# Three unused tiles that move the big tiles' addresses in a hybrid mixer and expert-choice kernel

## The chip, the cores and the metric

The kernel runs on one core of a Trainium2 chip. The metric is the device time of one execution in microseconds (us), the median of several.

## The reference

One layer of a latent backbone: 2048 tokens of 1024 channels, float32 throughout. A modulation vector comes from `c`; then a gated short convolution (the "mixer") and sixteen SwiGLU experts, each of which picks its own 256 tokens.

```python
m_l = (silu(c) @ ada_w + ada_b)
sh1, sc1, g1, sh2, sc2, g2 = jnp.split(m_l, 6, axis=-1)
hl  = rms_norm(x, norm_g[0]) * (1 + sc1) + sh1
gate_b, gate_c, v = jnp.split(hl @ w_in, 3, axis=-1)             # 1024 -> 3 x 1024
lat = x + g1 * ((gate_b * dwconv3(gate_c * v, conv)) @ w_out)
h2  = rms_norm(lat, norm_g[1]) * (1 + sc2) + sh2
aff = softmax(h2 @ w_router)                                     # 16 experts
g, idx = top_k(aff.T, 256)
xs  = h2[idx]                                                    # per expert 256 x 1024
ys  = ((silu(xs @ w_gate) * (xs @ w_up)) @ w_down) * g
out = lat + g2 * scatter_add(ys, idx)
```

## The kernel before

Every large product is made of three passes of TensorE in the type fp32r: an operand is split into a high part (a rounded copy, made by ScalarE) and a low part (what is left, a subtraction on VectorE), and high x high, high x low and low x high are added up in PSUM. In a matmul one operand is stationary (loaded into the array by a weight load, 128 columns here), the other is moving (streamed through it, one column after another).

**Weights.** All weights come in pieces of 512 KB. SyncE's queue loads a piece into one of three `raw` buffers (line 182), ScalarE writes the high half of a `ws` tile (L198), VectorE the low half (L208). There are 8 `ws` tiles of 8192 bytes a partition.

**Start** (0 to 50 us of the span). Columns of `ada_w` are loaded into `hl` buffers (L399), x into `xt` buffers, the first weights in halves (L226).

**Input projection** (to about 600 us), `in_mm`, lines 436, 437 and 439: two passes over 8 channel tiles, in each two quarters of the tokens, and for each of 8 slices `k` nine matmuls: 2 x 8 x 2 x 8 x 9 = 2304 of 512 columns. Moving is the token tile `hl`, stationary is a 128-column slice of `ws`.

**Output projection** (to about 825 us), `out_mm`, lines 641, 642 and 644: 16 token blocks x 8 slices x 6 = 768 matmuls of 512 columns. Here `ws` is moving, and stationary is `hl` (the `vh` and `vl` of the code take buffers of the tag `hl`). In its shadow stands the router (`router_mm`, lines 708 and 709): 32 weight columns of `rts`, 128 moving columns of `hl`.

**Routing** (825 to about 970 us) is a chain of small steps on VectorE, ScalarE and TensorE.

**Experts** (to the end). `gate_up`, lines 1010, 1012 and 1014: per expert 384 matmuls of 256 columns, moving is `xT` (the gathered tokens, transposed), stationary is `ws`; 6144 in all. `down`, lines 1032 to 1034: per expert 96 matmuls of 512 columns, moving is `ws`, stationary is `hT`; 1536 in all.

**Where tiles lie.** A pool gives its tiles places in each partition of the on-chip memory, one behind another in the order in which their names first appear, each rounded up to 32 bytes. The pools stand in the order `consts`, `weights` (`raw`, `ws`), `small`, `mix`. `mix` holds `junk`, `carry`, then 16 buffers `hl` of 4096 bytes, 9 of the tag `b4` (`xt`, `aw`, `u`) of 4096, and 5 of the tag `m2` of 2080. When the mixer is done, the pools `route` and `moe` take the place of `mix`; `moe` begins with `ax` (two of 320 bytes), then `oh`, `xs`, `xT`, `hT`, `sg` and `ot`. No line of the kernel asks for an alignment. The instructions are issued in the order of the code; nothing schedules them anew.

Of the kernel before, what the change touches and what calls it, by code (L numbers as in the profile page):

```python
# [7 lines left out]
F32 = mybir.dt.float32  # L8
# [8 lines left out]
P = 128  # L17
# [23 lines left out]
def block_kernel(ctx: ExitStack, tc, x, c, ada_w, ada_b, norm_g, w_in, conv, w_out, router, wg, wu, wd, out):  # L41
    nc = tc.nc
    ctx.enter_context(tc.manual_schedule())
    consts = ctx.enter_context(tc.tile_pool(name="consts", bufs=1))
# [13 lines left out]
    nc.vector.tensor_scalar(identf, jp, 0.0, None, op0=ALU.is_equal)  # L58
    ones_f = consts.tile([P, P], F32, name="ones_f")
    nc.vector.memset(ones_f, 1.0)  # L60
    spacer = consts.tile([1, 1], F32, name="spacer")
    mhalf = consts.tile([P, 1], F32, name="mhalf")
    nc.gpsimd.memset(mhalf, -0.5)
# [284 lines left out]
    with tc.tile_pool(name="mix", bufs=1) as mix:  # L348
# [9 lines left out]

        junk = mix.tile([P, D], BF, name="junk")
        carry = mix.tile([P, KD, 3], F32, name="carry")  # L360
        nc.gpsimd.memset(carry, 0.0)

        hl, xq = {}, {}
# [575 lines left out]


    moe = ctx.enter_context(tc.tile_pool(name="moe", bufs=1, reuse_waits="tile"))
    out_rows = out.rearrange("b t d -> (b t) d")
    H = QT
    idx_of, gate_of, xT_of, hT_of, ot_of, scat = {}, {}, {}, {}, {}, {}
# [181 lines left out]
```

## Time and profile before

| what | value |
|---|---|
| median of 3 runs | 1983.34 us (1981.32 to 1986.35) |
| the profiled execution's own time | 1985.33 us |
| its span, first to last instruction | 1983.5 us |
| TensorE busy with matmuls | 1901.4 us, 96% of the span |
| VectorE, ScalarE, GpSimd busy | 57%, 38%, 15% |
| DMA, mean over the span | 174 GB/s |
| mean granted clock of TensorE | 0.982 of full speed |

Matmuls are pipelined: a row's own duration covers most of two of them. How fast a stream of them runs is read from the starts in the timeline: (start of a later matmul minus start of an earlier one) divided by the number of matmuls from the one to the other. Below this is called the pitch.

### The profile page before, as it was taken

How to read it: one execution, taken by the hardware profiler on the slowest of the kernel's cores; microseconds unless marked ns; L12 is line 12 of the kernel's file. 1: busy time of each engine (PE TensorE's matmuls, PEld its weight loads, DVE VectorE, ACT ScalarE, POOL GpSimd, SP SyncE). 2: the span in 40 equal slices, each digit the busy share in tenths (PEclk: the TensorE clock that was granted, in tenths of full speed). 3: DMA queues.
4: the chain of work that ended last, by engine and by line, in shares of the span. 5: the costliest groups of instructions: out<-in, count | busy, mean ns of one | idle time of the engine just before them, and what ended most of it. 6: DMA issues, size and time to landing. Idle time of an engine off the chain costs nothing.

```text
span 1983.5 us, 29691 instructions
## 1 busy us (share of the span) xinstructions
PE 1901.4 (96%) x11930; PEld 1669.5 (84%) x11930; DVE 1130.6 (57%) x1656; ACT 751.2 (38%) x1050; POOL 306.9 (15%) x521
## 2 busy tenths in 40 slices
PE   4999999999999999659999999999999999999998
PEld 3787788887788888549999999999999999999996
DVE  7544424344334666776665656656665666566653
ACT  3411126211123333345444544444444444444542
POOL 3310011101011222333211011101110110111001
PEclk8999999999999999869999999999999999999999
DMA  9443241433216443235677676767677766777674
GB/s 283 127 133 127 81 144 53 139 127 123 67 64 213 166 149 132 85 127 165 199 222 211 214 233 200 220 217 235 202 214 233 227 201 214 229 209 218 212 212 116
DMA packets 216573, 344.38 MB, mean 174 GB/s; under 512 B 12092, under 2 KB 94068, under 8 KB 216436
## 3 DMA queue, kind: packets, MB, share of 16 engines
q1 hardware_dynamic: 200468, 284.82, 44.6%
q0 software_dynamic: 15968, 57.68, 11.2%
q8 instruction: 93, 1.52, 0.3%
q14 instruction: 44, 0.36, 0.1%
HBM read 300.51 MB, written 41.94 MB: 173 GB/s over the span
## 4 chain that ended last, share of the span: by engine, by line
PE 92%; DVE 3%; DMA 2%; SPq 1%; issue 1%; ACT 1%; POOL 0%; POOLq 0%; DVEq 0%; ACTq 0%
PE pm L1010 11%; PE pm L1012 11%; PE pm L1014 11%; PE pm L436 9%; PE pm L437 9%; PE pm L439 9%; PE pm L1032 6%; PE pm L1034 6%; PE pm L1033 6%; PE pm L641 3%; PE pm L644 3%; PE pm L642 3%; PE pt L986 1%; SPq L399 1%; DVE hl L312 1%
## 5 line engine op out<-in xcount | busy, mean ns | idle before, releaser
L208 DVE TENSOR_TENSOR ws<-raw,ws 128x1024 fp32r<-128x1024 f32 x415 | 499.0, 1223 | 314.4 <-ACT ws L198 312.5
L198 ACT ACTIVATE ws<-raw 128x1024 fp32r<-128x1024 f32 x437 | 451.0, 1054 | 444.2 <-PE pm L1014 208.0
L1010 PE MATMUL pm<-xT,ws 128*128 128x256 f32 x2048 | 569.6, 278 | 0.0
L1012 PE MATMUL pm<-xT,ws 128*128 128x256 f32 x2048 | 567.7, 277 | 0.1
L1014 PE MATMUL pm<-xT,ws 128*128 128x256 f32 x2048 | 567.4, 277 | 0.0
L1012 PEld LDWEIGHTS pm<-xT,ws 128*128 128x128 f32 x2048 | 386.4, 189 | 1.7 <-DVE xT L989 0.4
L1010 PEld LDWEIGHTS pm<-xT,ws 128*128 128x128 f32 x2048 | 386.2, 189 | 1.2
L1014 PEld LDWEIGHTS pm<-xT,ws 128*128 128x128 f32 x2048 | 386.0, 189 | 0.0
L436 PE MATMUL pm<-hl,ws 128*128 128x512 f32 x768 | 311.2, 405 | 1.0 <-ACT hl L386 1.0
L437 PE MATMUL pm<-hl,ws 128*128 128x512 f32 x768 | 307.0, 400 | 0.0
L439 PE MATMUL pm<-hl,ws 128*128 128x512 f32 x768 | 222.7, 398 | 0.0
L1032 PE MATMUL pm<-ws,hT 128*128 128x512 f32 x512 | 203.8, 398 | 0.0
L1034 PE MATMUL pm<-ws,hT 128*128 128x512 f32 x512 | 201.5, 394 | 0.0
L1033 PE MATMUL pm<-ws,hT 128*128 128x512 f32 x512 | 200.0, 391 | 0.0
L436 PEld LDWEIGHTS pm<-hl,ws 128*128 128x128 f32 x768 | 146.4, 191 | 36.6 <-ACT hl L386 1.4
L437 PEld LDWEIGHTS pm<-hl,ws 128*128 128x128 f32 x768 | 146.4, 191 | 35.1 <-issue 1.0
L439 PEld LDWEIGHTS pm<-hl,ws 128*128 128x128 f32 x768 | 145.8, 190 | 35.8
L1058 POOL DMA_INDIRECT out_dram<-ot,idx x32 | 78.5, 2454 | 591.4 <-DVE ot L1052 587.4
L449 DVE TENSOR_TENSOR u<-cs,pm 128x512 f32<-128x512 f32 x32 | 22.5, 703 | 246.0 <-ACT cs L446 246.0
L446 ACT ACTIVATE cs<-pm 128x512 f32<-128x512 f32 x32 | 19.1, 597 | 346.8 <-issue 272.0
L1034 PEld LDWEIGHTS pm<-ws,hT 128*128 128x128 f32 x512 | 96.2, 188 | 20.7
L1033 PEld LDWEIGHTS pm<-ws,hT 128*128 128x128 f32 x512 | 96.3, 188 | 18.9
(267 smaller groups left out, 2026.8 us busy)
## 6 DMA issues: line engine op xcount, KB each, us to landing
raw<-in_moe_w_gate_dram SPq DMA_DIRECT2D x128, 512.0 KB, 4.4
raw<-in_moe_w_up_dram SPq DMA_DIRECT2D x128, 512.0 KB, 4.3
raw<-in_moe_w_down_dram SPq DMA_DIRECT2D x128, 512.0 KB, 4.6
raw<-in_sc_w_in_dram SPq DMA_DIRECT2D x45, 512.0 KB, 4.6
xt<-in_x_dram SPq DMA_DIRECT2D x32, 512.0 KB, 6.2
aw<-in_ada_w_dram SPq DMA_DIRECT2D x32, 512.0 KB, 6.5
hl<-in_ada_w_dram SPq DMA_DIRECT2D x32, 256.0 KB, 5.4
hl<-vscr SPq DMA_DIRECT2D x16, 512.0 KB, 5.0
```

The source lines that it names most:

```text
L198: nc.scalar.activation(t[:, 0], raws[n_high], AF.Copy)
L208: (eng or nc.vector).tensor_sub(t[:, 1, ..., s], raw[..., s], t[:, 0, ..., s].bitcast(F32))
L436: nc.tensor.matmul(ps[m], wh, t[:, 0], start=(k == 0), stop=False)
L437: nc.tensor.matmul(ps[m], wl, t[:, 0], start=False, stop=False)
L439: nc.tensor.matmul(ps[m], W(k, m)[0], t[:, 1], start=False, stop=(k == KD - 1))
L1010: nc.tensor.matmul(o, w[:, 0, j, c0], xT[:, 0, k], start=(k == 0 and f % 2 == 0), stop=False, skip_group_check=True)
L1012: nc.tensor.matmul(o, w[:, 0, j, c0], xT[:, 1, k], start=False, stop=False, skip_group_check=True)
L1014: nc.tensor.matmul(o, w[:, 1, j, c0], xT[:, 0, k], start=False, stop=(k == KD - 1), skip_group_check=True)
L1032: nc.tensor.matmul(ps[s], h, w[:, 0, j], start=(k == 0), stop=False)
L1033: nc.tensor.matmul(ps[s], h, w[:, 1, j], start=False, stop=False)
L1034: nc.tensor.matmul(ps[s], l, w[:, 0, j], start=False, stop=(k == KD - 1))
L1058: st = nc.gpsimd.indirect_dma_start(out=out_rows, out_offset=bass.IndirectOffsetOnAxis(ap=idx_of[e][:, s:s + 1], axis=0), in_=ots[s], in_o ...
```

## The change

Three tiles are allocated that nothing reads or writes: 128 bytes a partition in `consts`, 96 in `mix` behind `carry`, 320 at the head of `moe`.

```diff
     ones_f = consts.tile([P, P], F32, name="ones_f")
     nc.vector.memset(ones_f, 1.0)
+    consts.tile([P, 32], F32, name="pad")
     spacer = consts.tile([1, 1], F32, name="spacer")
...
         junk = mix.tile([P, D], BF, name="junk")
         carry = mix.tile([P, KD, 3], F32, name="carry")
+        mix.tile([P, 24], F32, name="mixpad")
         nc.gpsimd.memset(carry, 0.0)
...
     moe = ctx.enter_context(tc.tile_pool(name="moe", bufs=1, reuse_waits="tile"))
+    moe.tile([P, 80], F32, name="moepad")
     out_rows = out.rearrange("b t d -> (b t) d")
```

On every engine the built program has the same instructions in the same order as before, with the same waits on the same semaphores and the same values; only addresses differ, so no row of an order is shown. The first byte in a partition of what the text speaks of (of the first buffer of a tag; the further ones lie whole buffers of 4096, 8192 or 16384 bytes on, `sg` 2048, and every slice that a matmul takes begins a multiple of 512 bytes into its tile, those of `rts` apart):

| tile | before | its remainder by 512 | by 64 | after | by 512 |
|---|---|---|---|---|---|
| `identf` | 17024 | 128 | 0 | 17024 | 128 |
| `rts` | 24960 | 384 | 0 | 25088 | 0 |
| `raw` | 32640 | 384 | 0 | 32768 | 0 |
| `ws` | 44928 | 384 | 0 | 45056 | 0 |
| `hl` | 116000 | 288 | 32 | 116224 | 0 |
| `b4` (`xt`, `aw`, `u`) | 181536 | 288 | 32 | 181760 | 0 |
| `xs` | 131136 | 64 | 0 | 131584 | 0 |
| `xT` | 139328 | 64 | 0 | 139776 | 0 |
| `hT` | 172096 | 64 | 0 | 172544 | 0 |
| `sg`, `ot` | 204864, 208960 | 64 | 0 | 205312, 209408 | 0 |

## Rows read from the trace of the kernel before

**Rows 1.** The page: busy time of TensorE, and the span in 40 slices.
```profile
PE 1901.4 (96%) x11930; PEld 1669.5 (84%) x11930; DVE 1130.6 (57%) x1656; ACT 751.2 (38%) x1050; POOL 306.9 (15%) x521
...
PE   4999999999999999659999999999999999999998
...
PEclk8999999999999999869999999999999999999999
```
**Rows 2.** The page: the chain that ended last, by engine and line.
```profile
PE 92%; DVE 3%; DMA 2%; SPq 1%; issue 1%; ACT 1%; POOL 0%; POOLq 0%; DVEq 0%; ACTq 0%
PE pm L1010 11%; PE pm L1012 11%; PE pm L1014 11%; PE pm L436 9%; PE pm L437 9%; PE pm L439 9%; PE pm L1032 6%; PE pm L1034 6%; PE pm L1033 6%; PE pm L641 3%; PE pm L644 3%; PE pm L642 3%; PE pt L986 1%; SPq L399 1%; DVE hl L312 1%
```
**Rows 3.** Busy time by stretch (the line of names says the columns).
```profile
core 0: us, PE busy (x) PEld busy (x) DVE busy (x) ACT busy (x) POOL busy (x), PEclk, DMA share, GB/s
...
100.00:200.00 100.00, 100.00 (x426) 79.75 (x425) 45.12 (x57) 17.43 (x22) 10.19 (x25) 1.00 0.40 135
...
615.00:820.00 205.00, 205.00 (x1116) 164.87 (x1114) 131.59 (x239) 63.28 (x151) 52.11 (x160) 1.00 0.43 150
830.00:870.00 40.00, 8.59 (x36) 5.48 (x36) 35.23 (x120) 15.63 (x42) 19.82 (x14) 0.50 0.38 122
...
1500.00:1700.00 200.00, 200.00 (x1507) 187.21 (x1507) 123.56 (x146) 91.70 (x107) 21.95 (x15) 1.00 0.72 220
```
**Rows 4.** Groups by line: TensorE, one line of each product (count; mean ns).
```profile
L1010 PE MATMUL pm<-xT,ws 128*128 128x256 f32 x2048 | 569.6, 278 | 0.0
...
L436 PE MATMUL pm<-hl,ws 128*128 128x512 f32 x768 | 311.2, 405 | 1.0 <-ACT hl L386 1.0
...
L1032 PE MATMUL pm<-ws,hT 128*128 128x512 f32 x512 | 203.8, 398 | 0.0
...
L641 PE MATMUL pm<-ws,hl 128*128 128x512 f32 x256 | 106.2, 415 | 0.0
```
**Rows 5.** Timeline of TensorE, input projection: start us, duration us; 45 matmuls between.
```profile
400.49 0.40 PE L436 MATMUL pm<-hl,ws 128*128 128x512 f32 x1
...
411.03 0.39 PE L436 MATMUL pm<-hl,ws 128*128 128x512 f32 x1
```
**Rows 6.** Timeline of TensorE, output projection: 12 matmuls between.
```profile
703.08 0.39 PE L641 MATMUL pm<-ws,hl 128*128 128x512 f32 x1
...
705.88 0.39 PE L641 MATMUL pm<-ws,hl 128*128 128x512 f32 x1
```
**Rows 7.** Timeline of TensorE, an expert's `down`: 18 matmuls between.
```profile
1576.29 0.39 PE L1032 MATMUL pm<-ws,hT 128*128 128x512 f32 x1
...
1580.41 0.39 PE L1032 MATMUL pm<-ws,hT 128*128 128x512 f32 x1
```
**Rows 8.** Timeline of TensorE, an expert's `gate_up`: 60 matmuls between.
```profile
1549.20 0.28 PE L1010 MATMUL pm<-xT,ws 128*128 128x256 f32 x1
...
1556.00 0.28 PE L1010 MATMUL pm<-xT,ws 128*128 128x256 f32 x1
```
**Rows 9.** Timeline of TensorE, the router: 14 matmuls between.
```profile
712.41 0.22 PE L709 MATMUL plt<-hl,rts 128*32 128x128 f32 x1
...
713.25 0.23 PE L709 MATMUL plt<-hl,rts 128*32 128x128 f32 x1
```
**Rows 10.** Groups by line: the split of `raw` into `ws`.
```profile
L208 DVE TENSOR_TENSOR ws<-raw,ws 128x1024 fp32r<-128x1024 f32 x415 | 499.0, 1223 | 314.4 <-ACT ws L198 312.5
L198 ACT ACTIVATE ws<-raw 128x1024 fp32r<-128x1024 f32 x437 | 451.0, 1054 | 444.2 <-PE pm L1014 208.0
```
**Rows 11.** Lines 631 and 630, the same split inside `hl` (ns: min/median/max).
```profile
L631 DVE TENSOR_TENSOR hl<-hl x16: 1215/1225/1226, 603.1 to 806.6; 128x1024 fp32r<-128x1024 f32 x16
...
L630 ACT ACTIVATE hl<-hl x16: 1052/1053/1061, 602.0 to 805.5; 128x1024 fp32r<-128x1024 f32 x16
```
**Rows 12.** Busy time by stretch of 10 us, in the start (columns as Rows 3).
```profile
10.00:20.00 10.00, 2.74 (x10) 2.00 (x11) 6.59 (x13) 7.38 (x13) 4.99 (x9) 1.00 1.08 317
...
40.00:50.00 10.00, 7.67 (x29) 6.29 (x30) 9.90 (x24) 2.01 (x3) 2.74 (x2) 0.72 1.16 305
```
**Rows 13.** DMA issues: KB each, median us from issue to landing.
```profile
raw<-in_moe_w_gate_dram SPq DMA_DIRECT2D x128, 512.0 KB, 4.4
...
hl<-in_ada_w_dram SPq DMA_DIRECT2D x32, 256.0 KB, 5.4
...
raw<-in_sc_w_in_dram SPq DMA_DIRECT2D x6, 256.0 KB, 5.4
```

## The prediction

> **What bounds the kernel now.** I read the page first. TensorE is busy with matmuls for 96% of the span, and the slices show it at 9 tenths or more everywhere but in the first, in two in the middle and in the last, with the granted clock at its upper level, 2.4 GHz, in the same slices [rows 1]. The chain that ended last says the same: 92% of it is TensorE, and twelve lines, the matmuls of the four products, hold nearly all of that [rows 2]. The busy times by stretch then show that the dense stretches have no holes: 100.00 of 100 us, 205.00 of 205, 200.00 of 200, at clock 1.00 [rows 3]. So a change is worth what it does to the matmul stream there; VectorE, ScalarE and the DMA queues are waited for only in the start and in the routing, where the clock falls to 0.50 [rows 3].
>
> A busy share of 100% doesn't say that the stream runs as fast as it could. The timeline does. At 2.4 GHz, one column a cycle, 512 columns take 213.3 ns, 256 take 106.7 and 128 take 53.3. The starts give these pitches:
>
> - Input projection, 512 columns: (411.03 - 400.49) / 45 = 234.2 ns [rows 5].
> - Output projection, 512 columns: (705.88 - 703.08) / 12 = 233.3 ns [rows 6].
> - `down`, 512 columns: (1580.41 - 1576.29) / 18 = 228.9 ns [rows 7].
> - `gate_up`, 256 columns: (1556.00 - 1549.20) / 60 = 113.3 ns [rows 8], which is 226.7 for 512.
> - Router, 128 columns: (713.25 - 712.41) / 14 = 60.0 ns [rows 9].
>
> None reaches one column a cycle, and three streams of the same instruction shape run at two rates, 234 and 229. What parts them? Not the other engines: the experts' stretch has the most of them (DMA 0.72, 220 GB/s, VectorE busy 124 of 200 us) and the shorter pitch; the projection's has less (0.40, 135 GB/s, 45 of 100) and the longer one [rows 3]. Not the clock, which is 1.00 in all three. Not the moving operand alone: output projection and `down` both stream `ws` at remainder 384 by 512, and differ in the stationary tile, `hl` (32 past a multiple of 64) against `hT` (a multiple of 64). The input projection has the same `hl` on the moving side. So both slow streams read a tile that lies 32 bytes off a multiple of 64, and both quicker ones read none. That is a correlation over four cases, and I build on it.
>
> **The change part by part.** It adds no instruction, takes none away, and moves no wait; three allocations cost nothing at run time. Nothing is queued differently on any engine, SP and POOL among them. What can change is how long an instruction takes at its new address.
>
> - *TensorE.* By the correlation the projections lose at least what parts them from `down`: 2304 x (234.2 - 228.9) = 12.2 us and 768 x (233.3 - 228.9) = 3.4 us [rows 4 to 7]. That is 15.6 us, the small value. But `down` also changes, from 384 and 64 to 0 and 0, and its nearest quicker row is `gate_up`, at 226.7 for the same columns. If all streams of 512 columns come to that rate: 2304 x 7.5 = 17.4, 768 x 6.7 = 5.1, 1536 x 2.2 = 3.4, together 25.9 us. I take this value and not the small one, since after the change no operand of any stream lies worse by 64, 128 or 256 than those of `gate_up` do now. For `gate_up` itself and the router I take nothing: the router's moving tile is `hl`, and its excess over one column a cycle, 6.7 ns, is the same as `gate_up`'s, so this part seems to hang on no address. Bounds: from below a loss, worked out under the rivals; from above the whole excess, 2304 x 20.9 + 768 x 20.0 + 1536 x 15.6 + 6144 x 6.7 = 129 us.
> - *VectorE and ScalarE.* The same split of 1024 columns takes 1223 and 1054 ns on `raw` and `ws`, at remainder 0 by 64 [rows 10], and 1225 and 1053 on `hl`, at 32 [rows 11]. I cost these engines at nothing. Even 10 ns on each split would lie beneath TensorE's stream.
> - *DMA.* Past the start the loads lie under TensorE; a load of a weight piece lands in 4.4 us [rows 13]. In the start they don't: the 16 DMA engines are full (shares 1.08 and 1.16) while TensorE is busy 2.74 and 7.67 us of 10 [rows 12]. Two kinds of load there have the same size and the same runs of 512 bytes, one to `hl` (remainder by 256: 32), one to `raw` (128), and both land in 5.4 us [rows 13]. So I take nothing, with 1 us either way for some 40 us in which they bound.
>
> The Trainium skill's page "DMA: Bandwidth & Descriptors", section "How a descriptor splits into AXI transactions", says that a run which doesn't start at a multiple of 256 bytes costs extra beats. For 512 bytes from 32 past one that is 17 beats against 16, as an estimate from that page 6% of the start's 40 us, 2.5 us of gain instead of nothing. It speaks of reads, and the two equal landings neither bear it out nor refute it.
>
> Sum: the profiled execution took 1985.33 us; less 25.9 that is 1959.4. The median of the runs lies 2.0 below the profiled execution, so 1957 to 1959; I say 1958.
>
> **The rivals.**
>
> *Only a fixed 6.7 ns is left (bigger gain).* If address stalls are all that parts 512 columns from the excess that router and `gate_up` show, 512 columns would take 213.3 + 6.7 = 220.0: 2304 x 14.2 + 768 x 13.3 + 1536 x 8.9 = 57 us, so 1928. For it: that excess is equal at 128 and 256 columns. Against it: `down` has operands at multiples of 64 and still shows 15.6. The Trainium skill, "TensorE: Matmul & The Clock Gate", section "Wait — 56ns, not 53.3ns?", goes further: it measured (on bf16) columns / 2.4 GHz plus about 2.5 ns at full clock. No row of this trace is that quick; as an estimate by that page every stream would fall to 215.8 and 109.2, a gain of 101 us, 1884. I give this rival 0.20, a third of it to gains beyond 70 us.
>
> *Nothing happens.* The pitch could hang on the pattern of the products (which operand is repeated, which accumulator is next) and not on addresses; then 1983, within 6 us. For it: the correlation has four cases that differ in more than addresses. Against it: an output row and a `down` row are the same in shape and in their moving tile. 0.17.
>
> *Slower: the two reads of a matmul collide.* TensorE reads the moving operand while it loads the next stationary one. Before, their starts differ by 96 bytes in the projections and by 320 in `gate_up` and `down`, taken by 512; after, by 0 everywhere. If reads that keep step at one remainder get in each other's way, `down` and `gate_up` would fall to the rate of the slowest stream here: 1536 x 5.3 = 8 us, and 6144 x (117.1 - 113.3) = 23 us, output projection 1: 32 us, 2015. For it: no stream of the trace has equal remainders, so nothing excludes it; sizes are all powers of two. Against it: loads of weights and streams start at different times, so equal starts needn't mean equal places at one time. If the projections gain their 22.5 us nevertheless, the sign turns where `gate_up` passes 113.3 + 22.5 / 6.144 = 117.0 ns; if they gain nothing, at its first tenth of a ns. 0.21.
>
> **How the numbers follow.** About 0.3% (6 us) is what a measurement of this kernel can tell from no change. The forecast (gain 10 to 40 us, so 1944 to 1974) has 0.42, which with the bigger gain makes faster 0.62; same 0.17; slower 0.21. The likeliest one's own range is 1944 to 1974. For 8 in 10, I go down past the 220 ns case (1928) to 1912, where some 0.08 is left below, and up past no change to 1996, where some 0.1 is left above.
>
> **What would show it.** In the changed kernel's timeline: 45 matmuls of the input projection in 10.2 us and not 10.54, 12 of the output projection in 2.72 and not 2.80, 18 of `down` in 4.08 and not 4.12, `gate_up` still at 113.3. The starts of the stages move with them: the experts begin some 22 us earlier, and the stretch from there to the end is some 3 shorter. VectorE's and ScalarE's durations stay within 5 ns, the start within 2 us. The prediction is wrong if `gate_up`, a third of the chain [rows 2], moves much: 1 ns of its pitch is 6.1 us. It is wrong in its step too if the projections gain while `hl` tiles turn out not to be what mattered.

## The result, and the profile after

The changed kernel is 0.7% slower: a median of 1998.95 us (1994.77 to 1999.9, 4 runs) against 1983.94 us (1981.32 to 1986.35) of the kernel before, a ratio of 1.0072, 95% interval 1.0052 to 1.0091. I had forecast 1958, with 1912 to 1996 as the range. The profiled execution is the quickest of the four: 1994.77 us, span 1993.0, granted clock 0.985.

The page after the change, in its lines on busy time, the chain that ended last by engine and by line, and the groups of the split and of one `gate_up` and one input-projection line:

```profile
PE 1914.7 (96%) x11930; PEld 1702.5 (85%) x11930; DVE 1128.3 (57%) x1656; ACT 750.3 (38%) x1050; POOL 309.7 (16%) x521
...
PE 93%; DVE 4%; issue 1%; ACT 1%; DMA 1%; POOL 0%; SPq 0%; POOLq 0%; DVEq 0%; ACTq 0%
PE pm L1013 12%; PE pm L1015 12%; PE pm L1017 12%; PE pm L438 8%; PE pm L441 8%; PE pm L439 8%; PE pm L1035 6%; PE pm L1036 6%; PE pm L1037 6%; PE pm L643 3%; PE pm L646 3%; PE pm L644 3%; PE pt L989 1%; DVE acc L416 1%; DVE hl L313 1%
...
L209 DVE TENSOR_TENSOR ws<-raw,ws 128x1024 fp32r<-128x1024 f32 x415 | 498.3, 1224 | 334.4 <-ACT ws L199 333.8
L199 ACT ACTIVATE ws<-raw 128x1024 fp32r<-128x1024 f32 x437 | 449.9, 1054 | 461.6 <-PE pm L1017 262.5
...
L1013 PE MATMUL pm<-xT,ws 128*128 128x256 f32 x2048 | 581.1, 284 | 0.2 <-ACT xT L991 0.2
...
L438 PE MATMUL pm<-hl,ws 128*128 128x512 f32 x768 | 305.3, 397 | 0.9 <-ACT hl L388 0.9
```

The bound is where it was. TensorE is 96% of the span and 93% of the chain, and the number of matmuls is the same. Set beside [rows 2, 4], the two kinds of work have moved in opposite directions: each `gate_up` line now has 12% of the chain and not 11, each input-projection line 8% and not 9. The mean of one matmul moved the same way, 278 to 284 ns in `gate_up` and 405 to 397 in the input projection. The splits of the weights take what they took in [rows 10].

In the busy times by stretch, one 100 us piece of the input projection and 200 us of the experts (columns as [rows 3]) are as full as before and have the same clock of 1.00. They hold 439 matmuls in place of 426, and 1464 in place of 1507:

```profile
100.00:200.00 100.00, 100.00 (x439) 82.11 (x438) 44.34 (x55) 17.47 (x22) 9.98 (x25) 1.00 0.42 140
...
1500.00:1700.00 200.00, 200.00 (x1464) 188.23 (x1462) 119.52 (x140) 87.59 (x101) 21.96 (x15) 1.00 0.70 212
```

The pitch, the distance from one start to the next, comes from the timeline of TensorE (start us, duration us). Four stretches, with 45, 12, 60 and 15 matmuls between the two rows of each:

```profile
399.97 0.39 PE L438 MATMUL pm<-hl,ws 128*128 128x512 f32 x1
...
410.17 0.39 PE L438 MATMUL pm<-hl,ws 128*128 128x512 f32 x1
...
644.34 0.39 PE L643 MATMUL pm<-ws,hl 128*128 128x512 f32 x1
...
647.06 0.39 PE L643 MATMUL pm<-ws,hl 128*128 128x512 f32 x1
...
1544.24 0.28 PE L1013 MATMUL pm<-xT,ws 128*128 128x256 f32 x1
...
1551.44 0.28 PE L1013 MATMUL pm<-xT,ws 128*128 128x256 f32 x1
...
1644.12 0.39 PE L1035 MATMUL pm<-ws,hT 128*128 128x512 f32 x1
...
1647.52 0.39 PE L1035 MATMUL pm<-ws,hT 128*128 128x512 f32 x1
```

Input projection 10.20 / 45 = 226.7 ns (was 234.2), output projection 2.72 / 12 = 226.7 (was 233.3), `down` 3.40 / 15 = 226.7 (was 228.9), `gate_up` 7.20 / 60 = 120.0 (was 113.3). So every stream of 512 columns came to exactly the rate that I had forecast, and `gate_up`, which I had left alone, lost 6.67 ns a matmul in these stretches. As a sum over all matmuls: 2304 x 7.56 = 17.4, 768 x 6.7 = 5.1 and 1536 x 2.2 = 3.4 us gained, 6144 x 6.67 = 41.0 us lost, net 15.0 us lost. The medians differ by 15.0 too, but that the two agree so well is in part luck: the starts that follow show no loss in the first two experts, and without their 768 matmuls of `gate_up` the loss is 5376 x 6.67 = 35.9 us and the net some 10.

The router's pitch stayed where it was, with 14 matmuls in 0.84 us, 60.0 ns:

```profile
693.76 0.23 PE L711 MATMUL plt<-hl,rts 128*32 128x128 f32 x1
...
694.60 0.22 PE L711 MATMUL plt<-hl,rts 128*32 128x128 f32 x1
```

The starts in the two timelines show where along the span it happened. These rows are the last matmul of the input projection, the first of `gate_up`, the first of expert 2 and the last of `down`, first in the kernel before:

```profile
603.52 0.86 PE L439 MATMUL pm<-hl,ws 128*128 128x512 f32 x3
...
876.01 0.56 PE L1010 MATMUL pm<-xT,ws 128*128 128x256 f32 x1
...
1005.14 0.28 PE L1010 MATMUL pm<-xT,ws 128*128 128x256 f32 x1
...
1974.27 0.40 PE L1034 MATMUL pm<-ws,hT 128*128 128x512 f32 x1
```

and in the changed kernel:

```profile
586.35 0.84 PE L441 MATMUL pm<-hl,ws 128*128 128x512 f32 x3
...
855.50 0.39 PE L1013 MATMUL pm<-xT,ws 128*128 128x256 f32 x1 [0.15 <-ACT xT L991]
...
981.96 0.28 PE L1013 MATMUL pm<-xT,ws 128*128 128x256 f32 x1
...
1983.92 0.39 PE L1037 MATMUL pm<-ws,hT 128*128 128x512 f32 x1
```

The changed kernel is 17.2 us ahead at the end of the input projection, 20.5 at the first `gate_up`, 23.2 at expert 2, and 9.7 behind at the end. I had forecast the experts' begin some 22 us earlier and the stretch from there to the end some 3 shorter; that stretch is 30.2 longer. From expert 2 on each expert costs 384 x 6.67 - 96 x 2.2 = 2.35 us more, 14 x 2.35 = 32.9, and 23.2 + 9.7 is 32.9. The first two experts lost nothing. Their stretch, first in the kernel before and then in the changed one (columns as [rows 3]):

```profile
876.00:1005.14 129.14, 123.09 (x957) 117.07 (x957) 86.66 (x182) 67.63 (x120) 31.51 (x15) 0.97 0.53 170
```

```profile
855.50:981.96 126.46, 122.43 (x955) 116.85 (x956) 86.08 (x182) 67.42 (x120) 31.55 (x15) 1.00 0.54 175
```

TensorE stands idle there for 6.1 us before and for 4.0 after, the granted clock is 0.97 and 1.00, and before, too, most of their `gate_up` was slow: in the second half of expert 1 the median of its eight groups of 24 matmuls is 117.8 ns. So this execution ends 9.65 us later where the medians say 15.0; the other three executions were not traced, and where their extra 4 to 5 us lie stays open. A hint is `all64` below, with the same pitches and a span that is 3.8 us longer (1996.8 against 1993.0): its first two experts take 128.91 us and not 126.46, which is 2.4 of the 3.8.

### The profile page after: what moved, and what is told of

Same layout as the page of the kernel before. It is cut to its first block, busy times and chain, and to the rows that moved or that the text cites. A ratio compares the mean times of both kernels' runs of the same rounds, so it can differ in the third digit from the quotient of the medians.

```text
span 1993.0 us, 29691 instructions
## 1 busy us (share of the span) xinstructions
PE 1914.7 (96%) x11930; PEld 1702.5 (85%) x11930; DVE 1128.3 (57%) x1656; ACT 750.3 (38%) x1050; POOL 309.7 (16%) x521
## 4 chain that ended last, share of the span: by engine, by line
PE 93%; DVE 4%; issue 1%; ACT 1%; DMA 1%; POOL 0%; SPq 0%; POOLq 0%; DVEq 0%; ACTq 0%
PE pm L1013 12%; PE pm L1015 12%; PE pm L1017 12%; PE pm L438 8%; PE pm L441 8%; PE pm L439 8%; PE pm L1035 6%; PE pm L1036 6%; PE pm L1037 6%; PE pm L643 3%; PE pm L646 3%; PE pm L644 3%; PE pt L989 1%; DVE acc L416 1%; DVE hl L313 1%
## 5 line engine op out<-in xcount | busy, mean ns | idle before, releaser
L209 DVE TENSOR_TENSOR ws<-raw,ws 128x1024 fp32r<-128x1024 f32 x415 | 498.3, 1224 | 334.4 <-ACT ws L199 333.8
L199 ACT ACTIVATE ws<-raw 128x1024 fp32r<-128x1024 f32 x437 | 449.9, 1054 | 461.6 <-PE pm L1017 262.5
L1013 PE MATMUL pm<-xT,ws 128*128 128x256 f32 x2048 | 581.1, 284 | 0.2 <-ACT xT L991 0.2
L1015 PE MATMUL pm<-xT,ws 128*128 128x256 f32 x2048 | 579.6, 283 | 0.3 <-DVE xT L992 0.3
L1017 PE MATMUL pm<-xT,ws 128*128 128x256 f32 x2048 | 579.5, 283 | 0.0
L1015 PEld LDWEIGHTS pm<-xT,ws 128*128 128x128 f32 x2048 | 393.0, 192 | 1.7 <-DVE xT L992 0.5
L1013 PEld LDWEIGHTS pm<-xT,ws 128*128 128x128 f32 x2048 | 393.0, 192 | 1.4 <-ACT xT L991 0.2
L1017 PEld LDWEIGHTS pm<-xT,ws 128*128 128x128 f32 x2048 | 393.0, 192 | 0.0
L438 PE MATMUL pm<-hl,ws 128*128 128x512 f32 x768 | 305.3, 397 | 0.9 <-ACT hl L388 0.9
L439 PE MATMUL pm<-hl,ws 128*128 128x512 f32 x768 | 301.1, 392 | 0.0
L441 PE MATMUL pm<-hl,ws 128*128 128x512 f32 x768 | 217.2, 391 | 0.0
L451 DVE TENSOR_TENSOR u<-cs,pm 128x512 f32<-128x512 f32 x32 | 22.5, 704 | 231.1 <-ACT cs L448 231.1
L1037 PEld LDWEIGHTS pm<-ws,hT 128*128 128x128 f32 x512 | 96.1, 188 | 20.5
```

The source lines that it names most:

```text
L199: nc.scalar.activation(t[:, 0], raws[n_high], AF.Copy)
L209: (eng or nc.vector).tensor_sub(t[:, 1, ..., s], raw[..., s], t[:, 0, ..., s].bitcast(F32))
L438: nc.tensor.matmul(ps[m], wh, t[:, 0], start=(k == 0), stop=False)
L439: nc.tensor.matmul(ps[m], wl, t[:, 0], start=False, stop=False)
L441: nc.tensor.matmul(ps[m], W(k, m)[0], t[:, 1], start=False, stop=(k == KD - 1))
L1013: nc.tensor.matmul(o, w[:, 0, j, c0], xT[:, 0, k], start=(k == 0 and f % 2 == 0), stop=False, skip_group_check=True)
```

## The experiments

Each kernel moves tiles by the sizes of the unused ones, and by a fourth, `hTpad`, allocated in the pool `moe` after the first loads, which moves `hT` against `xT`. Diffs are against the changed kernel. I give a kernel's starts as four remainders by 512: (`ws`, `hl`, `xT`, `hT`). Before is (384, 288, 64, 64), the change (0, 0, 0, 0).

**First: equal remainders, or each tile's own?** Theory A in the expectations is the clash of the two reads of a matmul. Theory B says that each operand's own remainder counts, Theory C that `ws` alone does. The kernel before took 1984.64 us on the chip of these four.

All four at 64 (`all64`):
```
-    consts.tile([P, 32], F32, name="pad")
+    consts.tile([P, 48], F32, name="pad")
```


> The changed kernel with the pad in consts 64 bytes longer, so that ws, hl, xT and hT all start 64 past a multiple of 512: equal remainders as in the changed kernel, but not 0. Theory A (a matmul's two reads clash when the moving and the stationary tile have the same remainder by 512): gate_up stays at 120.0 ns, total about 1999. Theory B (xT itself must not start at a multiple of 512): gate_up back to 113.3, total about 1958. Both: the streams of 512 columns stay at 226.7, if multiples of 64 are what they need.

`xT` alone at 64 (`xt64`), timed in three rounds:
```
-    moe.tile([P, 80], F32, name="moepad")
+    moe.tile([P, 96], F32, name="moepad")
...
+    moe.tile([P, 112], F32, name="hTpad")
```


> The changed kernel with xT moved back to 64 past a multiple of 512, all other operands of matmuls (ws, hl, hT) left at multiples of 512. Theories A and B both: gate_up 113.3 ns, the streams of 512 columns 226.7, so 6144 x 6.7 = 41 us less than the changed kernel: about 1958. Theory C (the slower gate_up comes from ws at a multiple of 512, not from xT): gate_up stays at 120, total about 1999.

The third unused tile left out, which gives (0, 0, 192, 192) (`no_moepad`):
```
-    moe.tile([P, 80], F32, name="moepad")
```


> The changed kernel without the third pad: ws and hl at multiples of 512, xT and hT at 192. Theories A and B: gate_up 113.3. down tells what the streams of 512 columns gained from: if a multiple of 64 is enough, it stays at 226.7; if equal remainders of both operands made it quicker, it goes back to about 229. Total 1958 to 1962.

`hl` at 32, `xT` and `hT` at 256 (`hl32_moe256`):
```
-        mix.tile([P, 24], F32, name="mixpad")
+        mix.tile([P, 32], F32, name="mixpad")
...
-    moe.tile([P, 80], F32, name="moepad")
+    moe.tile([P, 144], F32, name="moepad")
```


> The changed kernel with hl at 32 and xT and hT at 256 past a multiple of 512, ws at 0. If the 32 bytes off a multiple of 64 were what slowed the projections, they go back to 233 to 234 ns (+22 us against the changed kernel). Theory A with a period of 512: gate_up 113.3, with a period of 256: 120. Theory B: 113.3. down: 226.7 if a multiple of 64 is enough.

Measured: `all64` 1998.57 us, with `gate_up` at 120.0 as in the changed kernel, so the remainders themselves did nothing:

```profile
1409.28 0.28 PE L1013 MATMUL pm<-xT,ws 128*128 128x256 f32 x1
...
1416.48 0.28 PE L1013 MATMUL pm<-xT,ws 128*128 128x256 f32 x1
```

`xt64` gave 1985.75 us, a ratio of 1.0012 (1.0002 to 1.0022), `gate_up` at 117.8: moving `xT` away from `ws` by 64 gives a third of the loss back, where A and B expected all of it (113.3) and C none (120). `no_moepad` gave 1964.1, with `gate_up` back at 113.3 and `down` at 228.9. `hl32_moe256` gave 2011.98: the projections fell back to 233.3, which the prediction's reason (`hl` 32 off a multiple of 64) and a distance of 32 both explain, while `gate_up` and `down`, 256 apart from `ws`, stayed at 120.0 and 226.7. The input projection of that kernel, 45 matmuls in 10.50 us:

```profile
400.04 0.40 PE L438 MATMUL pm<-hl,ws 128*128 128x512 f32 x1
...
410.54 0.39 PE L438 MATMUL pm<-hl,ws 128*128 128x512 f32 x1
```

So equal starts are bad for `gate_up` and good for 512 columns, and 256 apart is the same as equal. What seems to count is the distance, start of the moving operand less start of the stationary one, by 256 (A2 in what follows): 0 gives 226.7 and 120.0.

**Second: only the distance?** Four kernels that put the same distance at other remainders, or other distances. The kernel before on that chip: 1985.37.

All four at 32 (`all32`), 32 bytes off a multiple of 64, which my prediction's reason calls slow:
```
-    consts.tile([P, 32], F32, name="pad")
+    consts.tile([P, 40], F32, name="pad")
```


> The changed kernel with everything 32 bytes further: ws, hl, xT and hT all at 32 past a multiple of 512. Theory A2 (distance): all distances stay 0, so the projections and down keep 226.7, gate_up 120.0, total about 1999. Theory B, the correlation of the prediction (a tile 32 off a multiple of 64 is slow): the projections and down go back to 233 to 234, total about 2029.

`hl`, `xT` and `hT` at 128 (`all128`), all multiples of 64:
```
-        mix.tile([P, 24], F32, name="mixpad")
+        mix.tile([P, 56], F32, name="mixpad")
...
-    moe.tile([P, 80], F32, name="moepad")
+    moe.tile([P, 112], F32, name="moepad")
```


> The changed kernel with hl, xT and hT at 128 past a multiple of 512, ws at 0. Theory A2 (what counts is the distance of the moving start from the stationary start by 256): every stream is at a distance of 128, which no run had yet. If it is better the further apart the two are, gate_up 113.3 or less and the streams of 512 columns below 226.7, so below 1960. Theory B (each operand's own remainder): all are multiples of 128 but none of xT, hl, hT a multiple of 256; gate_up 113.3 as for 192, streams of 512 columns 226.7.

`hl` at 192, `xT` at 224, `hT` at 64 (`hl192_xt224_ht64`):
```
-        mix.tile([P, 24], F32, name="mixpad")
+        mix.tile([P, 72], F32, name="mixpad")
...
-    moe.tile([P, 80], F32, name="moepad")
+    moe.tile([P, 136], F32, name="moepad")
...
+    moe.tile([P, 88], F32, name="hTpad")
```


> The changed kernel with hl at 192, xT at 224, hT at 64 past a multiple of 512, ws at 0. Distances moving minus stationary by 256: input projection 192, output projection 64, gate_up 224, down 192. Theory A2: output projection 228.9 (as down at 64), gate_up between 113.3 (192) and 120 (0), the two at 192 new. Theory B: the projections stay at 226.7, since 192 is a multiple of 64.

The third unused tile alone on the kernel before (`moepad_only`): (384, 288, 384, 384), the projections untouched:
```
-    consts.tile([P, 32], F32, name="pad")
...
-        mix.tile([P, 24], F32, name="mixpad")
```


> The kernel before with the third pad alone: ws stays at 384 and hl at 288, xT and hT come to 384 as well. Theory A2: gate_up 120.0 (+41 us), down 226.7 (-3 us), the projections as before, so about 2022. Theory B (a multiple of 512 is what slows gate_up): gate_up stays at 113.3, total about 1984.

Measured: `all32` 1997.41 us, with all four pitches of the changed kernel. Its input projection, 45 matmuls in 10.20 us:

```profile
400.11 0.39 PE L438 MATMUL pm<-hl,ws 128*128 128x512 f32 x1
...
410.31 0.39 PE L438 MATMUL pm<-hl,ws 128*128 128x512 f32 x1
```

`all128`, where every tile is a multiple of 64, has 512 columns at 232 to 233 and took 2012.84. Its input projection, 45 matmuls in 10.45 us:

```profile
400.07 0.39 PE L438 MATMUL pm<-hl,ws 128*128 128x512 f32 x1
...
410.52 0.39 PE L438 MATMUL pm<-hl,ws 128*128 128x512 f32 x1
```

With `all32` this refutes "32 off a multiple of 64 is slow" from both sides. It also refutes the guess that further apart is better: by 256, two starts can be no further apart than 128, and `gate_up` has 118.5 to 118.8. `hl192_xt224_ht64` took 2009.76: the input projection and `down` at distance 192 have 233.3, the output projection at 64 has 228.9. `moepad_only` took 2018.8, the slowest of all: the projections stay at 234.3 and 233.3, and `gate_up` has 120.0 with `ws` and `xT` both at 384:

```profile
1430.30 0.28 PE L1011 MATMUL pm<-xT,ws 128*128 128x256 f32 x1
...
1437.50 0.28 PE L1011 MATMUL pm<-xT,ws 128*128 128x256 f32 x1
```

**Third: the distance of `gate_up`.** The kernels keep `ws`, `hl` and `hT` at 0 and put `xT` elsewhere; before on that chip: 1983.67. The two numbers are the sizes of `moepad` and `hTpad`:
```
-    moe.tile([P, 80], F32, name="moepad")
+    moe.tile([P, 128], F32, name="moepad")
...
+    moe.tile([P, 80], F32, name="hTpad")
```
for `xt192`, 120 and 88 for `xt160`, 104 and 104 for `xt96`, 88 and 120 for `xt32`.

> The changed kernel with xT at 192 past a multiple of 512, and ws, hl and hT at 0: each stream at the best distance seen so far. Theory A2 (distance by 256): gate_up 113.3, the streams of 512 columns 226.7, 6144 x 6.7 = 41 us less than the changed kernel, 1958, and 1.3% faster than before. Theory B was left with nothing after the tile set at 32 throughout. If the pitch of gate_up hung on something else that moved with hT, the total would stay above 1964.

> As xt192 with xT at 160. Theory A2 has no value for gate_up at 160; the 512-column streams were slow at every distance that is no multiple of 64, so 117 to 119 is expected here, about 1981 to 1993.

> As xt192 with xT at 96: by the same reasoning 117 to 119 for gate_up, about 1981 to 1993. A pitch below 113.3 would mean that a better place than 192 exists.

> As xt192 with xT at 32: by the same reasoning 117 to 119 for gate_up, about 1981 to 1993.

Measured: `xt32` 1979.64 us (116.7 ns), `xt96` 1998.79 (120.0, more than expected), `xt160` 1990.18 (118.7). `xt192` missed its forecast of 1958: in five rounds it took 1983.89, a ratio of 1.0 (0.9991 to 1.0009). Its `gate_up` has 117.8 from expert 2 on and 113.3 only in a part of the first two, although its distance is that of `no_moepad` and of the kernel before. 60 matmuls in 7.06 us:

```profile
1401.05 0.28 PE L1013 MATMUL pm<-xT,ws 128*128 128x256 f32 x1
...
1408.11 0.28 PE L1013 MATMUL pm<-xT,ws 128*128 128x256 f32 x1
```

So the distance is not all. The kernel with 113.3 comes to each `gate_up` from a `down` at distance 64, `xt192` from one at distance 0.

**Fourth: what decides between 113.3 and 117.8?** Before on that chip: 1984.0. `two_pads` is `no_moepad` again, timed in five rounds. `xt192_ht64` has `moepad` 128 and `hTpad` 96, `xt64_ht192` 96 and 32. `xt192_kick` is `xt192` with one matmul of 64 columns at the head of each `gate_up` from expert 2 on, whose result the next matmul overwrites:
```
+        if e > 1:
+            nc.tensor.matmul(ps[0][0][:, 0, 0:64], ws_of[w_moe[0, e, fh, 0]][:, 0, 0, 0:P], xT[:, 0, 0, 0:64],
+                             start=True, stop=True, skip_group_check=True)
```


> The changed kernel without the third pad once more, now timed: ws and hl at 0, xT and hT at 192. As in its first look: projections 226.7, gate_up 113.3, down 228.9; 1964 us, ratio to the kernel before 0.990.

> xT at 192, hT at 64, ws and hl at 0. down then runs at a distance of 192 (233.3 ns). If the stream ahead chooses gate_up's rhythm, this is a third way in, and may give either 113.3 or 117.8; total 1972 or 1999. If it takes equal places of xT and hT to have 113.3, it is 117.8.

> xT at 64, hT at 192, ws and hl at 0: down is entered and left as in the kernel without the third pad (distance 64, 228.9 ns). If the distance of gate_up's own operands still sets its rhythms, it stays at 117.8 (as with hT at 0), about 1989; if the entry alone decides, 113.3, about 1964.

> The kernel with xT at 192 and hT at 0, and one matmul of 64 columns more at the head of each gate_up from the third expert on (its product is overwritten at once). If the entry decides, some or all blocks fall into 113.3 instead of 117.8, down to about 1960; if they stay at 117.8, about 1986, and the entry is not shown to matter.

Measured: `xt192_kick` 1965.2 us, 18.7 below `xt192`. In all 28 halves of `gate_up` from expert 2 on, the first full matmul starts 204 or 205 ns ahead of the second, four gaps of 114 to 123 follow, and from the sixth matmul on the pitch is 113.3. The added matmul, the first, second and sixth full ones, and then 60 in 6.80 us:

```profile
1391.54 0.19 PE L1000 MATMUL pm<-xT,ws 128*128 128x64 f32 x1
1391.57 0.36 PE L1016 MATMUL pm<-xT,ws 128*128 128x256 f32 x1
1391.78 0.28 PE L1018 MATMUL pm<-xT,ws 128*128 128x256 f32 x1
...
1392.25 0.28 PE L1020 MATMUL pm<-xT,ws 128*128 128x256 f32 x1
...
1394.40 0.28 PE L1016 MATMUL pm<-xT,ws 128*128 128x256 f32 x1
...
1401.20 0.28 PE L1016 MATMUL pm<-xT,ws 128*128 128x256 f32 x1
```

`xt192_ht64` took 1980.7; from expert 2 on its even experts have 113.3 and its odd ones 117.8 (but 113.3 in the last half of the last), with the same remainders in the same code. The last matmul of `down` starts 235 to 236 ns before the first of `gate_up` where 113.3 follows, 229 to 230 where 117.8 does. `xt64_ht192` took 1990.69, with `gate_up` at 117.8 in spite of a `down` at distance 64: the entry matters at distance 192, and the two kernels at 64 show no such thing. So at 192 the stream has two rhythms, each of which, from expert 2 on, lasts to the end of its half, and how the stream is entered picks one. (128 has two as well: in `all128` three halves have 120.0, the others 118.5 to 118.8.) What in the entry does it, the runs don't show.

`two_pads`, the change without its third tile, is the best kernel of all: 1962.78 us (1962.39 to 1964.56), a ratio of 0.9896 (0.988 to 0.9913). Its `gate_up`, 60 matmuls in 6.80 us:

```profile
1391.14 0.28 PE L1012 MATMUL pm<-xT,ws 128*128 128x256 f32 x1
...
1397.94 0.28 PE L1012 MATMUL pm<-xT,ws 128*128 128x256 f32 x1
```

It keeps 17.4 + 5.1 = 22.5 us of the projections and gives up only `down`'s 3.4; the medians differ by 21.2.

All pitches together, from start differences in dense stretches as above (ns):

| Distance by 256 | 512 columns | where | 256 columns, `gate_up` | where |
|---|---|---|---|---|
| 0 | 226.7 | after, `all64`, `all32`; `down` in `moepad_only`, `hl32_moe256` | 120.0 | the same five |
| 32 | 233.3 | input projection, `hl32_moe256` | 116.7 | `xt32` |
| 64 | 228.9 | `down` of before, `no_moepad`, `xt64_ht192`; output projection, `hl192_xt224_ht64` | 117.8 | `xt64`, `xt64_ht192` |
| 96 | 233.3 | output projection, before | 120.0 | `xt96` |
| 128 | 232 to 233 | `all128` | 118.5 to 118.8 (120.0 in three halves of an expert) | `all128` |
| 160 | 234.3 | input projection, before | 118.7 | `xt160` |
| 192 | 233.3 | `down`, `xt192_ht64`; input projection and `down`, `hl192_xt224_ht64` | 113.3 or 117.8 | before, `no_moepad`, `xt192_kick`; `xt192`; both in `xt192_ht64` |
| 224 | 233.3 | output projection, `hl32_moe256` | 118.3 | `hl192_xt224_ht64` |

Three products with different tiles and operands swapped share one column for 512, so it isn't one tile or line that does it. The router, with 128 columns, shows nothing of the kind: its slices of `rts` lie 128 bytes apart, so its distance (`hl` less `rts`) is 160 and 32 in turn before, 0 and 128 after, and its pitch is 60.0 both times.

## Why the prediction was wrong

**The step that failed** is the one on TensorE that reads "For `gate_up` itself and the router I take nothing", with its reason "this part seems to hang on no address". The router and `gate_up` had the same 6.7 ns over one column a cycle, and I took that for a fixed part. It was not: `gate_up` can have anything from 6.7 to 13.3 ns at the same shape, by where `xT` lies against `ws`. By the pitches the term is +41.0 us for all 6144 matmuls, and +35.9 in the traced execution, where the first two experts lost nothing; either is more than all the gains together. The equal excess of two streams was a coincidence of one layout.

**The other terms of the sum** were right in size: 17.4, 5.1 and 3.4 forecast, and the same three from the pitches. By the starts, 17.2 us were gained up to the end of the input projection and 3.3 from there to the first `gate_up`. `two_pads` shows the first two alone on the chip.

**Their reason was wrong.** I put the slow projections down to `hl` lying 32 past a multiple of 64. `all32` has every tile there and is as quick as the change; `all128` has none there and is slow. My four cases differed in distance too: 160 and 96 in the slow ones, 64 in `down`. I worked out starts of 96 and 320 apart for the rival, and didn't try them as the explanation. That the gain came out right is luck: the change brought all distances to 0, which happens to be the best place for 512 columns.

**The rival whose outcome came true** is *the two reads of a matmul collide*, for `gate_up` alone; whether reads collide, no run shows. I had priced it at 117.1 ns, the rate of the slowest stream; it was 120.0, past the 117.0 at which I had put the turn of the sign. For `down` it was the wrong way round: I said 234 at equal starts, and equal starts gave 226.7. My reason against it, that loads and streams start at different times, was no reason: `gate_up` did slow down at equal starts.

**The other rivals.** *Only a fixed 6.7 ns is left* would need 220.0 for 512 columns; no layout went below 226.7. The Trainium skill's "TensorE: Matmul & The Clock Gate", section "Wait — 56ns, not 53.3ns?", with about 2.5 ns over the columns, is that of no stream here: the quickest have 13.3 over 213.3, and 6.7 over 106.7. The gap that it explains is that of bf16 matmuls, and these are of another type. *Nothing happens* fell with the pitches. The router's pitch stayed at 60.0, as forecast.

**VectorE and ScalarE**: forecast within 5 ns, measured 1 ns and 0 (1224 and 1054). **The start**: forecast within 2 us. The 145th matmul of the input projection stands at 84.30 before and at 82.69 after, in the other kernels at 82.6 to 85.8, so nothing that the layout explains shows there.

**Why the distance counts is not shown.** The trace has the load of the next weights busy under the stream for 85% of the span, so the read of the moving operand and that of the next stationary one do run at the same time, and a meeting of the two would depend on the distance of their starts and on their phase, as the two rhythms at 192 do. That is argued only: no run took the loads away from the stream.

## What to carry to other kernels

When TensorE has no holes, compare the pitch of each stream with its columns before believing that it is at its limit, and vary the distance between the two operands' starts one stream at a time: here that alone moved a whole kernel from 1962.78 to 2018.8 us. A layout that suits one shape needn't suit another (0 is best for 512 columns and, with 96, worst for 256), so "align everything" is no rule. A number that two streams share in one layout is not a constant until a second layout has shown it.

## What was not expected of the hardware

- At 2.4 GHz the quickest 512-column stream has 226.7 ns, 544 cycles, which is 512 + 32. `gate_up` has 288 at distance 0 and 272 at its best, 256 + 32 and 256 + 16.
- At distance 192 the same instructions with the same remainders have two lasting rhythms, 113.3 and 117.8 ns, and one added matmul of 64 columns per half moves the stream from the slower to the quicker.
- The load of 256 KB to `hl` landed sooner with `hl` at a multiple of 256: 4.7 us in the changed kernel, against 5.4 [rows 13].

```profile
hl<-in_ada_w_dram SPq DMA_DIRECT2D x32, 256.0 KB, 4.7
...
raw<-in_sc_w_in_dram SPq DMA_DIRECT2D x6, 256.0 KB, 5.5
```

In the ten others with `hl` at 0 it is 4.4 to 4.9, in the six others with `hl` at 32, 64, 128, 192 or 288 it is 5.2 to 5.9. The rule that the prediction named, from the Trainium skill's "DMA: Bandwidth & Descriptors", section "How a descriptor splits into AXI transactions", would have the same direction, but it is told of reads, and these are writes to SBUF. The load to `raw`, of the same size and in the same stage, did not follow: `raw` moved from 128 past a multiple of 256 to 0, and its load landed in 5.4 us before and in 5.5 after. So the alignment of the tile as the cause is not shown. The start as a whole shows no gain from it (the 145th matmul above).
